# Modulation weights read by thirds: one ahead of each layer, two in the router stage and in the last attention

## The chip, the cores and the metric

The kernel runs on one core of a Trainium2 chip. The metric is the device time of one execution in microseconds (us), median of the runs. Engines work side by side, each through its own fixed list of instructions: PE (matmuls), DVE (vector), ACT (activations), POOL and SP, which here issue DMAs.

## The reference

Two transformer blocks on 256 tokens of width 1024, in fp32. The first mixes retention and sliding-window attention, then runs a mixture of 32 experts (top-1 group, top-2 experts) and a small gated embedding (PLE). The second block has two layers; each is modulated by a vector that comes from a condition c (for the tokens) and from c_ctx (for the context):

```
for i in range(DEPTH_2):
    mod = (s_c @ w_mod[i] + b_mod[i])[:, None, :]
    sh1, sc1, gt1, sh2, sc2, gt2 = jnp.split(mod, 6, axis=-1)
    ...
    h = modulate(rms_norm_2(x, g_norm1[i]), sh1, sc1)
    p = h @ w_in[i]
    ...  # three attention-like branches, merged to mix
    x_new = x + gt1 * mix
    x_new = x_new + gt2 * squared_relu_mlp(modulate(rms_norm_2(x_new, g_norm2[i]), sh2, sc2), ...)
```

w_mod[i] has 1024 rows and 6144 columns, 25 MB. Its first third of columns holds sh1 and sc1, needed at the start of a layer; the second gt1 (needed when the mixed branches are added) and sh2; the last sc2 and gt2, needed in the MLP.

## The kernel before

Weights are read from HBM by SP in pieces of up to 512 KB into a pool of 8 tiles called raw. Since products are made to fp32 accuracy, a piece is split by ACT (wh, L199) and DVE (wl, L200), three tiles each, and multiplied in three matmuls: L257 to L259 with 256 columns, L285 to L287 with 512. SP issues its loads in one order, and a load waits until its raw tile is free.

The instructions are written by Python code, and a list scheduler then fixes the order of each engine. A generator can be run beside the main code: `beside(steps, every)` (L202) enters it, each weight piece of the main code calls `advance` (L207), and one step is written for every `every` pieces; `drain` writes what is left. Pieces stand a little ahead in priority (AHEAD), modulation matmuls more (CLUSTER).

The modulation is such a generator, `w_mod` (L755). For each third of the columns it holds one PSUM tile of 512 columns and makes eight steps, one for each 128 rows: two raw tiles of 128x1024 are loaded (L764), and four matmuls (L769) multiply the two condition columns (padded to 32) with a quarter each, on a quarter of the array's columns each (`tile_position`). The weights are used as they are, without a split. A bias step (L775, L780) follows, then the copy out of PSUM and four small DMAs on POOL to a scratch in DRAM (modscr, L786). Once all thirds of a layer are there, two DMAs bring the columns back as modcol (L788). `rows` (in `Layer`) makes from modcol the gains A of both norms; `gate_row` reads gt1 and gt2 from modscr.

Stages in order: block1_mix and block1_out with w_out (the opening, with modulation of layer 0 beside block1_mix, one step for 1.25 pieces, PSUM tag cs); the router, and the start of the context layer `cl` (its projections na_k and na_v); the experts with the rest of the context layer; PLE and the attention of x0 (with all of layer 1's modulation beside them, every 1.5, later 2.5 pieces, tag pd); x0's MLP; x1's attention (the last attention) with the context's keys and values beside it; x1's output and MLP. In the attention, scores and transposes take PSUM tiles by turns from ps, cs and cd; dense products use pd and cd.

The router: w_out's residual gives x; L351 (ACT) sums its squares, Newton steps and L820 (DVE) make the normalised rows, L827 (PE) transposes them, L832 gives the logits; the choice of experts follows on DVE, then the lists for the scatter and gather on POOL, and L985 is the first transposition of gathered rows for an expert.

Of the kernel before, what the change touches and what calls it, by code (L numbers as in the profile page):

```python
# [15 lines left out]
ALU = mybir.AluOpType  # L16
# [51 lines left out]


WEIGHTS = (8, 3, 3)  # L70
MOD_EVERY = 1.25
AHEAD = 80
LANE = 192
EDGE = 160
# [3 lines left out]
KV_EVERY = 5.0  # L78
MOE_EVERY = 2.68
CTX_EVERY = (1.0, 1.2)  # L80
MOD1_EVERY = (1.5, 2.5)
CHAIN_EVERY = (1.0, 0.8)
ACTS_E = {"a8": 6, "a4": 6, "a2": 4, "tg": 2}
ACTS_C = {"a8": 4, "a4": 5, "a2": 3, "tg": 2, "pr": 1, "pt": 1, "lr": 1}
# [79 lines left out]
class Build:  # L164
# [252 lines left out]
    def run_all(self):  # L417
        nc, tc, i = self.nc, self.tc, self.i
        with ExitStack() as ctx:
            self.P = ctx.enter_context(tc.tile_pool(name="keep", bufs=1))  # L420
            self.W = ctx.enter_context(tc.tile_pool(name="weights", bufs=1))
            self.Dr = ctx.enter_context(tc.tile_pool(name="scr", bufs=1, space=DRAM))
            self.psum = ctx.enter_context(tc.tile_pool(name="psum", bufs=1, space=PSUM))
            self.ident = self.P.tile([128, 128], F32, name="ident")
            self.sums = self.P.tile([128, 2, 2, 2], F32, name="sums").rearrange("p s t c -> s p t c")
            self.ints = self.P.tile([128, 16], I32, name="ints")
            self.x = self.P.tile([128, 2, 1024], F32, name="xres")
            self.mod_input()
            for t in range(2):
                nc.sync.dma_start(self.x[:, t], i["x"][0, t * 128:t * 128 + 128])  # L430
            nc.sync.dma_start(self.ident, i["ident"])
            self.modcol = self.P.tile([128, 2, 2, 6, 8], F32, name="modcol")
            self.modscr = [self.Dr.tile([2, 6144], F32, name=f"modscr{l}") for l in range(2)]
            self.kvscr = [self.Dr.tile([128, 5120], F32, name=f"kvscr{l}") for l in range(2)]
            self.ctxscr = self.Dr.tile([128, 2048], F32, name="ctxscr")
            self.X = ctx.enter_context(tc.tile_pool(name="xT", bufs=1))
            ca = ctx.enter_context(ExitStack())
            self.slots = ca.enter_context(tc.tile_pool(name="slots", bufs=1))
            cl = Layer(self, None, 0, "ctx")
            with ExitStack() as ce:  # L440
                early = Stream(self, ce, "e", ACTS_E, ["pd"], ["ps", "cd"])
                mod = self.beside(self.w_mod(early, "cs", 0), MOD_EVERY)
                mh = self.block1_mix(early)
                self.layer_consts(early)
                self.gple = self.gain_col("ple_gate_norm_g")
                self.drain(mod)
                self.loads, self.ready = self.expert_loads(), []
                cl.rows(early)
                self.block1_out(early, mh)
                cl.turn(early)  # L450
            self.dump("x1", self.x)
            cs = Stream(self, ca, "c", ACTS_C, ["cd"], ["cs"])
            cl.st = cs
            with ExitStack() as cr:
                route = Stream(self, cr, "r", {}, ["pd"], ["ps"])
                self.router(route, cs)
                for _ in range(2):
                    self.fetch()
                cl.start()
            experts = self.beside(self.moe(cs), MOE_EVERY)  # L460
            cl.finish()
            self.drain(experts)
            self.dump("x2", self.x)
            self.mst = cs
            mod = self.beside(self.w_mod(None, "pd", 1), MOD1_EVERY[0])
            self.ple(cs)
            ca.close()
            st = Stream(self, ctx, "b", ACTS_B, ["pd", "cd"], ["ps", "cs"])
            self.mst = st
            mod[1] = MOD1_EVERY[1]  # L470
            self.dump("x3", self.x)
            for tag, n in (("ss1", 1), ("nm", 16), ("ny", 16), ("nt", 16)):
                st.small([128, n], tag=tag, bufs=2 if tag == "ss1" else 8)
            self.na_mask = st.pool.tile([128, 64], F32, name="namask")
            nc.sync.dma_start(self.na_mask, i["na_mask"])
            self.W2 = st.pool
            self.W2.tile([128, 1024], F32R, name="wh", tag="wh", bufs=1)
            st.pad(LANE)
            kv = Layer(self, st, 1, "kv")
            x0 = Layer(self, st, 0, "x")  # L480
            x0.rows(st)
            x0.turn(st)
            x0.start()
            x0.finish(lambda: self.drain(mod), kv)
            self.dump("x4", self.x)
            x1 = Layer(self, st, 1, "x")
            x1.rows(st)
            kv.na_v()
            x1.turn(st)
            kv.na_k_end()  # L490
            chain = self.beside(kv.mla_kv(), KV_EVERY)
            x1.start()
            self.drain(chain)
            x1.finish()

    def layer_consts(self, st):
        nc, i, P = self.nc, self.i, self.P
# [254 lines left out]
        self.one = self.P.tile([1, 32], F32, name="one32")  # L752
        nc.vector.memset(self.one, 1.0)

    def w_mod(self, st, tag, l):  # L755
        nc, i = self.nc, self.i
        mm = nc.tensor.matmul
        for j in range(3):
            ps = self.psum.tile([128, 512], F32, name=tag, tag=tag, bufs=2)
            for k in range(8):  # L760
                wt = [self.weight(0) for _ in range(2)]
                for u in range(2):
                    c = j * 2048 + u * 1024
# [9 lines left out]
            for u in range(2):  # L773
                c = j * 2048 + u * 1024
# [9 lines left out]
            for g in range(4):  # L784
                c = (4 * j + g) * 512
                nc.gpsimd.dma_start(self.modscr[l][:, c:c + 512], ev[32 * g:32 * g + 2])  # L786
        for r in range(2):
            nc.gpsimd.dma_start(self.modcol[:, l, r], self.modscr[l][r].rearrange("(a p k) -> p a k", a=6, k=8))  # L788

    def router(self, st, act):  # L790
        nc, i = self.nc, self.i
# [23 lines left out]
        r = self.newton(st, self.sumsq(st, self.x), 2, 1.0 / D)  # L815
        lgT = one.tile([36, 256], F32, name="lgT")
        lps = st.dense()
        xn = act.a(8).rearrange("p (t k q) -> p t k q", t=2, k=8)
        for t in range(2):
            nc.vector.scalar_tensor_tensor(xn[:, t], self.x[:, t].rearrange("p (q k) -> p k q", k=8), r[:, t:t + 1],  # L820
# [2 lines left out]
        for j in range(4):  # L823
            ps = st.small_ps().rearrange("p (k t) -> p k t", k=2)
            for kk in range(2):
                for t in range(2):
                    nc.tensor.transpose(ps[:, kk, t * 128:t * 128 + 128], xn[:, t, 2 * j + kk], self.ident)  # L827
            hT = act.a(2).rearrange("p (k t) -> p k t", k=2)
            self.evac(hT, ps)
            for kk in range(2):  # L830
                k = 2 * j + kk
                mm(lps[:36, :256], wr[:, k], hT[:, kk], start=k == 0, stop=k == 7)  # L832
        nc.vector.tensor_copy(lgT, lps[:36, :256])
        lg = one.tile([128, 2, 36], F32, name="lg")
        ps = st.small_ps()
        for t in range(2):
            nc.tensor.transpose(ps[:, t * 36:t * 36 + 36], lgT[:, t * 128:t * 128 + 128], self.ident[:36, :36])
        nc.vector.tensor_tensor(lg, ps[:, :72].rearrange("p (t e) -> p t e", t=2),
                                br[:, None, :].to_broadcast([128, 2, 36]), op=ALU.add)
        tl = lambda shape, nm, dt=F32: one.tile(shape, dt, name=nm)  # L840
        gl = tl([128, 2, 8], "gl")
        nc.vector.memset(gl, -3.0e38)
# [43 lines left out]
        mm(ps[:, 1], tri[:, 1], M[:, 0], start=False, stop=True)  # L886
        mm(ps[:, 2], tri[:, 1], M[:, 0], start=True, stop=False)
        mm(ps[:, 2], tri[:, 1], M[:, 1], start=False, stop=True)
        rank = tl([128, 3, 32], "rank")
        nc.vector.tensor_copy(rank, ps[:, 0:3])  # L890
        cmax = tl([128, 1], "cmax")
# [5 lines left out]
        for t in range(2):  # L897
            for k in range(2):
                nc.vector.tensor_tensor_reduce(out=junk, in0=oh[:, t, k], in1=rank[:, t], scale=1.0, scalar=0.0,
                                               op0=ALU.mult, op1=ALU.add, accum_out=rk[:, t, k:k + 1])  # L900
# [26 lines left out]
        for g in range(8):  # L927
            for t in range(2):
                mm(ps[:, g:g + 1], S[:, t, 4 * g:4 * g + 4].rearrange("p e s -> p (e s)"), tok[:, t:t + 1],
                   start=t == 0, stop=t == 1)  # L930
        self.sti = self.ints[:, 5:13]
        nc.vector.tensor_copy(self.sti, ps[:, :8])

# [279 lines left out]
class Layer:  # L1213
# [74 lines left out]
    def rows(self, st):  # L1288
        nc, l, b = self.nc, self.l, self.b
        self.load_x(st)  # L1290
        mc = self.mc = b.modcol[:, l, self.r]
        self.gna, self.gm, self.gmt, self.gqc = (z[:, l] for z in (b.gna, b.gm, b.gmt, b.gqc))
        self.rope = b.rope if self.mode == "x" else None
        A = self.A = b.X.tile([128, 2, 8], F32, name="modA", tag="modA", bufs=3)
        for c in range(2):
            nc.vector.scalar_tensor_tensor(A[:, c], mc[:, 3 * c + 1], 1.0, b.g12[:, l, c], op0=ALU.add, op1=ALU.mult)
        self.xn = b.norm_rows(st, self.x, stats=self.mode == "x")

    def turn(self, st):
# [391 lines left out]
    def ffn(self, meanwhile=None):  # L1691
        nc, i, st, b, l = self.nc, self.i, self.st, self.b, self.l
        xn = b.norm_rows(st, self.x, stats=True)
        self.gate_row(5)
        if meanwhile:
            meanwhile()
        xT = b.turn(st, xn, mod=(self.A[:, 1], self.mc[:, 3]))
# [52 lines left out]
```

## Time and profile before

| | us |
|---|---|
| median of 3 runs | 1927.31 (1920.61 to 1930.31) |
| profiled execution | 1928.43 |
| its span in the trace | 1926.7 |
| PE busy | 1796.3 (93%) |
| DVE busy | 1243.7 (65%) |
| ACT busy | 919.0 (48%) |

The rows further down come from the trace of that one execution. A row of a window gives the busy time of each engine in the stretch, then the mean granted clock of PE (1 is full), the mean busy share of the DMA engines and what they moved. A row of waits adds up the idle time of an engine that ended with a given releaser. Matmuls are pipelined, so their records overlap: the pitch, from one start to the next, is what counts.

### The profile page before, as it was taken

What the parts mean: (1) busy time and instruction counts of PE and PEld (TensorE: products, weight loads), DVE (VectorE), ACT (ScalarE), POOL (GpSimd) and SP (SyncE); (2) the same over time, 40 slices, a digit from 0 to 9 for tenths busy, and PEclk for the clock granted to TensorE, in tenths of its full rate; (3) what the DMA queues carried; (4) which work ended last, traced back from release to release, by engine and by line L of the source; (5) the groups of instructions that cost most, each with busy time, mean ns of one, the idle gap of its engine ahead of it and who ended that gap; (6) DMA issues with size and microseconds to landing.
All of it is one profiled execution on the core that took longest, in us unless ns stands there. A gap on an engine that the chain in (4) does not pass through costs nothing. (4 is left out here: it accounts for less than half of the span.)

```text
span 1926.7 us, 32421 instructions
## 1 busy us (share of the span) xinstructions
PE 1796.3 (93%) x12572; PEld 1478.0 (77%) x12572; DVE 1243.7 (65%) x2324; ACT 919.0 (48%) x1432; POOL 214.3 (11%) x209
## 2 busy tenths in 40 slices
PE   5999878999999999988999989999999899998998
PEld 3678856777786877665777878799988888787998
DVE  3554656664567544455768596766688886866665
ACT  3433534563345433344535455655456555555443
POOL 3000111000110101100121110011100200010110
PEclk9999988999999999999999999999999999998999
DMA  8789847889999999977787753555567645254652
GB/s 277 257 309 289 269 146 236 299 289 334 334 344 361 324 366 333 341 271 247 254 241 208 225 165 100 164 179 193 197 184 225 172 126 165 72 195 143 197 189 95
DMA packets 277172, 448.82 MB, mean 233 GB/s; under 512 B 35582, under 2 KB 182380, under 8 KB 276568
## 3 DMA queue, kind: packets, MB, share of 16 engines
q1 hardware_dynamic: 266344, 417.30, 64.7%
q0 software_dynamic: 10672, 29.43, 5.2%
q8 instruction: 99, 1.62, 0.3%
q14 instruction: 57, 0.47, 0.1%
HBM read 430.77 MB, written 15.86 MB: 232 GB/s over the span
## 5 line engine op out<-in xcount | busy, mean ns | idle before, releaser
L200 DVE TENSOR_TENSOR wl<-raw,wh 128x1024 fp32r<-128x1024 f32 (+2 forms) x484 | 614.7, 1273 | 361.5 <-ACT wh L199 204.8
L199 ACT ACTIVATE wh<-raw 128x1024 fp32r<-128x1024 f32 (+2 forms) x484 | 505.3, 1047 | 561.6 <-PE pd L258 116.2
L259 PE MATMUL pd<-xT,wl 128*128 128x256 f32 x384 | 109.9, 286 | 5.6 <-DVE wl L200 5.6
L258 PE MATMUL pd<-xT,wh 128*128 128x256 f32 x384 | 109.9, 286 | 0.0
L257 PE MATMUL pd<-xT,wh 128*128 128x256 f32 x384 | 109.6, 285 | 0.3 <-DVE b_a L339 0.3
L259 PE MATMUL pd<-e_a,wl 128*128 128x256 f32 x288 | 81.8, 284 | 0.5 <-DVE wl L200 0.5
L257 PE MATMUL pd<-e_a,wh 128*128 128x256 f32 x288 | 82.0, 285 | 0.0
L995 PE MATMUL ps<-ew,m_heT 128*32 128x256 f32 x1024 | 75.6, 384 | 6.7 <-DMA ew<-in_w_exp_up_dram 5.6
L258 PE MATMUL cd<-xT,wh 128*128 128x256 f32 x288 | 81.5, 283 | 0.0
L258 PE MATMUL pd<-e_a,wh 128*128 128x256 f32 x288 | 81.4, 283 | 0.0
L259 PE MATMUL cd<-xT,wl 128*128 128x256 f32 x288 | 81.2, 282 | 0.1
L257 PE MATMUL cd<-xT,wh 128*128 128x256 f32 x288 | 81.2, 282 | 0.0
L259 PEld LDWEIGHTS pd<-xT,wl 128*128 128x128 f32 x384 | 73.5, 191 | 8.9 <-DVE wl L200 6.4
L258 PE MATMUL cd<-b_a,wh 128*128 128x256 f32 x280 | 77.7, 277 | 0.0
L257 PE MATMUL cd<-b_a,wh 128*128 128x256 f32 x280 | 77.7, 277 | 0.0
L259 PE MATMUL cd<-b_a,wl 128*128 128x256 f32 x280 | 77.5, 277 | 0.0
L257 PEld LDWEIGHTS pd<-xT,wh 128*128 128x128 f32 x384 | 73.2, 191 | 4.3 <-issue 3.1
L258 PEld LDWEIGHTS pd<-xT,wh 128*128 128x128 f32 x384 | 73.3, 191 | 2.9 <-issue 2.5
L285 PE MATMUL cd<-wh,xT 128*128 128x512 f32 (+2 forms) x208 | 73.3, 354 | 0.0
L286 PE MATMUL cd<-wl,xT 128*128 128x512 f32 (+2 forms) x208 | 72.6, 349 | 0.1
L287 PE MATMUL cd<-wh,xT 128*128 128x512 f32 (+2 forms) x208 | 72.4, 348 | 0.0
L1669 POOL TENSOR_TENSOR xres<-xres,b_a 128x512 f32<-128x512 f32 x24 | 37.5, 1561 | 304.5 <-DVE b_a L1667 304.5
(774 smaller groups left out, 5087.6 us busy)
## 6 DMA issues: line engine op xcount, KB each, us to landing
raw<-in_ffn_w_dram SPq DMA_DIRECT2D x192, 512.0 KB, 4.4
raw<-in_w_in_dram SPq DMA_DIRECT2D x168, 512.0 KB, 5.0
raw<-in_w_mod_dram SPq DMA_DIRECT2D x96, 512.0 KB, 5.8
ew<-in_w_exp_gate_dram SPq DMA_DIRECT2D x64, 512.0 KB, 7.7
ew<-in_w_exp_up_dram SPq DMA_DIRECT2D x64, 512.0 KB, 8.4
ew<-in_w_exp_down_dram SPq DMA_DIRECT2D x64, 512.0 KB, 7.5
raw<-in_w_out_dram SPq DMA_DIRECT2D x32, 512.0 KB, 5.5
raw<-in_w_in_dram SPq DMA_DIRECT2D x16, 504.0 KB, 4.3
```

Of the source, the lines that this page charges most:

```text
L199: self.nc.scalar.activation(h, src, AF.Copy)
L200: self.nc.vector.tensor_tensor(l, src, h.bitcast(F32), op=ALU.subtract)
L257: mm(ps, wh[:, s], xh[:, k], start=k == 0, stop=False)
L258: mm(ps, wh[:, s], xl[:, k], start=False, stop=False)
L259: mm(ps, wl[:, s], xh[:, k], start=False, stop=k == n - 1)
L285: mm(ps[t], xh[:, k, s], wh, start=k == 0, stop=False)
L286: mm(ps[t], xh[:, k, s], wl, start=False, stop=False)
L287: mm(ps[t], xl[:, k, s], wh, start=False, stop=k == K - 1)
L995: mm(pg[32 * e:32 * e + 32, u * 256:u * 256 + 256], heT[:, kh * 4 + k, 32 * e:32 * e + 32], ws[e][:, k], start=kh == 0 and k == 0, stop=kh ...
L1669: (nc.vector if stats else nc.gpsimd).tensor_tensor(xs, xs, tmp, op=ALU.add)
```

## The change

w_mod takes a list of thirds, and brings each third's modcol back with two small DMAs of its own. For layer 0, the first third is made beside block1_mix (a step for 4 pieces) and the other two beside the router and the start of the context layer (a step for 2, tag pd), for which the router calls `advance` at six places; they are drained after `cl.start()`. For layer 1, the first third is made beside PLE and x0 (a step for 7, tag cs), the others beside x1's attention (a step for 4, tag cs), drained in x1.finish before the output. The second norm's gain A[:, 1] is made in `ffn`. Lines behind L441 shift by 1 to 9.

```diff
-MOD_EVERY = 1.25
+MOD0_EVERY = (4.0, 2.0)
-MOD1_EVERY = (1.5, 2.5)
+MOD1_EVERY = (7.0, 4.0)
...
-                mod = self.beside(self.w_mod(early, "cs", 0), MOD_EVERY)
+                mod = self.beside(self.w_mod(early, "cs", 0, (0,)), MOD0_EVERY[0])
...
+            self.mst = cs
+            mod = self.beside(self.w_mod(None, "pd", 0, (1, 2)), MOD0_EVERY[1])
             with ExitStack() as cr:
...
                 cl.start()
+            self.drain(mod)
...
-            self.mst = cs
-            mod = self.beside(self.w_mod(None, "pd", 1), MOD1_EVERY[0])
+            mod = self.beside(self.w_mod(None, "cs", 1, (0,)), MOD1_EVERY[0])
...
-            mod[1] = MOD1_EVERY[1]
...
+            mod = self.beside(self.w_mod(None, "cs", 1, (1, 2)), MOD1_EVERY[1])
             x1.start()
             self.drain(chain)
-            x1.finish()
+            x1.finish(lambda: self.drain(mod))
...
-    def w_mod(self, st, tag, l):
+    def w_mod(self, st, tag, l, thirds):
...
-        for j in range(3):
+        for j in thirds:
...
-        for r in range(2):
-            nc.gpsimd.dma_start(self.modcol[:, l, r], self.modscr[l][r].rearrange("(a p k) -> p a k", a=6, k=8))
+            for r in range(2):
+                nc.gpsimd.dma_start(self.modcol[:, l, r, 2 * j:2 * j + 2],
+                                    self.modscr[l][r, 2048 * j:2048 * j + 2048].rearrange("(a p k) -> p a k", a=2, k=8))
...
         lps = st.dense()
+        self.advance(4.0)
...
+            if j % 2:
+                self.advance(2.0)
...
+        self.advance(4.0)
         tl = lambda shape, nm, dt=F32: one.tile(shape, dt, name=nm)
...
+        self.advance(2.0)
         rank = tl([128, 3, 32], "rank")
...
+        self.advance(2.0)
         self.sti = self.ints[:, 5:13]
...
-        for c in range(2):
-            nc.vector.scalar_tensor_tensor(A[:, c], mc[:, 3 * c + 1], 1.0, b.g12[:, l, c], op0=ALU.add, op1=ALU.mult)
+        nc.vector.scalar_tensor_tensor(A[:, 0], mc[:, 1], 1.0, b.g12[:, l, 0], op0=ALU.add, op1=ALU.mult)
...
+        nc.vector.scalar_tensor_tensor(self.A[:, 1], self.mc[:, 4], 1.0, b.g12[:, l, 1], op0=ALU.add, op1=ALU.mult)
```

SP's order where w_out ends and the context's projections begin. Before (in_w_out is w_out, the tiles of 128x2x512 of in_w_in are na_k's, those of 336 na_v's, in_w_exp_gate an expert's):

```order
L241 DMA raw<-in_w_out_dram 128x2x512 x2
L947 DMA ew<-in_w_exp_gate_dram 128x1024
L241 DMA raw<-in_w_out_dram 128x2x512
L947 DMA ew<-in_w_exp_gate_dram 128x1024 x2
L241 DMA raw<-in_w_in_dram 128x2x512 x3
L947 DMA ew<-in_w_exp_gate_dram 128x1024
L241 DMA raw<-in_w_in_dram 128x2x512
L947 DMA ew<-in_w_exp_gate_dram 128x1024
L241 DMA raw<-in_w_in_dram 128x3x336 x2
```

And in the changed kernel:

```order
L241 DMA raw<-in_w_out_dram 128x2x512 x2
L766 DMA raw<-in_w_mod_dram 128x1024 x16
L241 DMA raw<-in_w_in_dram 128x2x512
L777 DMA raw<-in_b_mod_dram 1x1024 x2
L766 DMA raw<-in_w_mod_dram 128x1024 x2
L241 DMA raw<-in_w_in_dram 128x2x512 x2
L766 DMA raw<-in_w_mod_dram 128x1024 x2
L241 DMA raw<-in_w_in_dram 128x2x512
L241 DMA raw<-in_w_in_dram 128x3x336
```

Sixteen modulation tiles now stand behind w_out, and more of them between those of na_k and na_v; the experts' gate tiles stand earlier.

PE's order at the same place in the changed kernel (e_a is w_out's other operand, the L393 rows are transposes of the context, xT is the context for na_k):

```order
L285 MATMUL pd<-wh,e_a_1983 128x512
L771 MATMUL pd<-raw,sT 32x512 x16
L286 MATMUL pd<-wl,e_a_1983 128x512
L287 MATMUL pd<-wh,e_a_1984 128x512
L393 MATMUL cd<-ident,e_a_2064 128x128
L393 MATMUL ps<-ident,e_a_2064 128x128 x4
L393 MATMUL cd<-ident,e_a_2064 128x128 x3
L771 MATMUL pd<-raw,sT 32x512 x4
L393 MATMUL cd<-ident,e_a_2064 128x128
L393 MATMUL ps<-ident,e_a_2064 128x128 x4
L771 MATMUL pd<-raw,sT 32x512 x12
L285 MATMUL cd<-wh,xT 128x512 x2
```

All eight steps of the second third stand there ahead of na_k, four of them ahead of w_out's last two matmuls; before, no modulation matmul stood behind block1_mix until PLE.

PE's order in the last attention of the changed kernel, in a dense product (wh and wl against xT), as one step of the last third stands there:

```order
L257 MATMUL pd<-xT,wh 128x256
L771 MATMUL cs<-raw,sT 32x512
L258 MATMUL pd<-xT,wh 128x256
L771 MATMUL cs<-raw,sT 32x512
L259 MATMUL pd<-xT,wl 128x256
L771 MATMUL cs<-raw,sT 32x512
L257 MATMUL pd<-xT,wh 128x256
L771 MATMUL cs<-raw,sT 32x512
L258 MATMUL pd<-xT,wh 128x256
```

The four matmuls of the step stand one by one between dense ones. Before, no modulation matmul stood in this stage.

## Rows read from the trace of the kernel before

**Rows 1.** The page: busy time, slices of PE and its clock.

```profile
PE 1796.3 (93%) x12572; PEld 1478.0 (77%) x12572; DVE 1243.7 (65%) x2324; ACT 919.0 (48%) x1432; POOL 214.3 (11%) x209
...
PE   5999878999999999988999989999999899998998
...
PEclk9999988999999999999999999999999999998999
```

**Rows 2.** Windows of 50 us: engines' busy time, clock, DMA share, GB/s.

```profile
0.00:50.00 50.00, 29.18 (x138) 20.07 (x139) 18.89 (x48) 17.71 (x27) 18.07 (x31) 0.93 0.90 282
...
250.00:300.00 50.00, 40.15 (x199) 31.71 (x198) 31.43 (x91) 17.82 (x29) 6.83 (x12) 0.86 0.44 134
```

**Rows 3.** Windows of 10 us.

```profile
40.00:50.00 10.00, 7.91 (x42) 7.62 (x43) 6.11 (x16) 3.39 (x6) 0.00 (x0) 0.66 1.01 386
50.00:60.00 10.00, 7.89 (x51) 5.30 (x50) 6.24 (x27) 5.32 (x9) 0.00 (x0) 0.83 0.82 303
...
270.00:280.00 10.00, 2.98 (x10) 1.81 (x11) 6.51 (x14) 2.33 (x5) 1.08 (x2) 0.50 0.39 138
```

**Rows 4.** Timeline, router: start, length, instruction, [idle before <- what ended it].

```profile
267.92 0.76 ACT L199 ACTIVATE wh<-raw 128x672 fp32r<-128x672 f32 x1 [1.71 <-PE cd L287]
268.59 1.04 ACT L351 ACTIVATE r_junk<-xres 128x1024 bf16<-128x1024 f32 x1
...
273.45 4.03 DVE L820 SCALAR_TENSOR_TENSOR c_a<-xres,r_ny,c_a 128x1024 f32<-128x1024 f32 x2
...
275.71 0.66 PE L827 MATMUL ps<-ident,c_a 128*128 128x128 f32 x2 [7.83 <-issue]
...
314.68 1.73 PE L985 MATMUL ps<-ident,m_he 128*128 128x128 f32 x7 [3.37 <-DMA m_he<-xnscr,ints]
```

**Rows 5.** Window of the last attention.

```profile
1443.00:1711.00 268.00, 253.17 (x1858) 223.84 (x1859) 209.71 (x489) 150.39 (x271) 30.54 (x22) 0.97 0.54 157
```

**Rows 6.** PE's waits in the last attention: total, times, longest.

```profile
PE cs L1652 <- ACT b_a L337: 3.5, 1, 3.5
PE cd L1140 <- DVE b_a L200: 2.9, 1, 2.9
...
PE cs L1326 <- ACT b_a L404: 2.3, 1, 2.3
```

**Rows 7.** Timeline of PE: a whole step, then lone matmuls between dense ones.

```profile
102.92 1.06 PE L769 MATMUL cs<-raw,sT 128*32 128x512 f32 x8
103.92 0.39 PE L258 MATMUL pd<-e_a,wh 128*128 128x256 f32 x1
...
886.91 0.39 PE L287 MATMUL cd<-wh,ew 128*128 128x512 f32 x1
887.14 0.40 PE L285 MATMUL cd<-wh,ew 128*128 128x512 f32 x1
887.47 1.04 PE L769 MATMUL pd<-raw,sT 128*32 128x512 f32 x2
...
888.87 1.04 PE L769 MATMUL pd<-raw,sT 128*32 128x512 f32 x2
```

**Rows 8.** Windows of the modulation matmuls L769 alone.

```profile
0.00:200.00 200.00, 27.48 (x192) 3.95 (x192) 0.97 0.86 281
850.00:1100.00 250.00, 35.75 (x192) 5.19 (x192) 0.98 0.76 237
```

**Rows 9.** PE's waits in the opening.

```profile
PE pd L285 <- ACT wh L199: 6.4, 3, 3.8
PE cs L769 <- DMA raw<-in_w_mod_dram: 5.6, 3, 3.2
```

**Rows 10.** PE's waits from 840 to 1100 us.

```profile
PE ps L393 <- ACT b_a L380: 6.6, 1, 6.6
PE pd L769 <- DMA raw<-in_w_mod_dram: 5.6, 6, 1.5
...
PE cs L1171 <- DVE b_aden L1159: 1.2, 1, 1.2
```

## The prediction

> **What bounds the kernel now.** I read the page's first two parts, then the windows, then the waits by stretch, then the places in order of time. PE is busy 93% of the span and its row of slices is lowest in the first slice and the sixth, where the clock is lower too [rows 1]. So time is PE work plus the places where PE waits, and each stage has its own kind of wait. The opening (0 to 257 us, the end of w_out) is where loads are short: 29.18 of the first 50 us are PE work while the DMA engines are .90 busy [rows 2]. From 250 to 300 the DMA share is .44, and PE has 40.15 of 50 us [rows 2]; in the ten us from 270 PE works 2.98 at a clock of .50 [rows 3]. The gap there is not a load: the router's transposes L827 come at 275.71, since the sum of squares L351 runs on ACT only at 268.59, right behind the last split of na_v's first group, and the normalised rows L820 on DVE take 4.03 us from 273.45 [rows 4]. The first expert work, L985, is at 314.68 [rows 4]. In the last attention (1443 to 1711) PE works 253.17 of 268 us at DMA .54 [rows 5]: 14.8 us of idle time, in short waits of at most 3.5 us [rows 6], and much room for loads.
>
> **What a modulation step costs.** A step is two tiles of 512 KB and four matmuls, one for each quarter of the array's columns. Where the four stand in a row they run together: eight records (two for a matmul) of 1.06 us in all, and the next dense matmul starts 1.00 us after the first [rows 7]. Where one stands alone between dense matmuls of 512 columns, the period is 888.87 - 887.47 = 1.40 us, of which the dense one takes 0.23 (its pitch just before); 1.17 us are left for one matmul [rows 7]. So a step broken in four costs 4.7 us, not 1.05, and what counts is not the matmuls, whose number stays 216, but the runs in which they stand. I counted these runs in the order of both kernels (a run of n costs n/4, rounded up). Before: 28 for layer 0, all in the opening, and 37 for layer 1, beside PLE and x0; 65, where 54 is the least. After: 16 in the opening, 20 in the router stage, 20 beside PLE and x0, 42 in the last attention; 98. The busy time agrees: 27.48 us for the 24 steps of layer 0 (without bias), 35.75 for those of layer 1 [rows 8].
>
> The row that prices the lone matmul is 1.04 us long and takes 1.17 of the engine's time [rows 7], so 0.13 us go beside it. The Trainium skill, TensorEngine Tiling (Array Packing), Key Properties, says that a change of tiling mode drains the engine, which is what a lone matmul between full-width ones asks for twice. By that rule the 0.13 is paid for each run, by the record alone it would be free; the 34 broken runs in the last attention come to 40 us by the one and 35 by the other. I take the measured period. The trace agrees in sign, and no run here shows the drain by itself.
>
> **Opening: -27 us (-18 to -36).** PE loses 28 runs of 1.05 = 29.4 us and gets 16: 6 whole and 10 broken, 6 x 1.05 + 10 x 1.17 = 18.0; -11. The waits for modulation tiles, 5.6 us, go, and so does most of ACT's waiting for dense tiles that stood behind them in SP's queue, 6.4 us seen at L285 [rows 9]; -11. The clock was .66 from 40 to 50 us and .83 from 50 to 60 [rows 3], behind such waits, which is (1 - .66) x 10 + 1.7 = 5.1 us of full clock lost; -5. The upper end has the queue as the bound: 32 fewer tiles of 512 KB would be worth more than PE's share of them. The lower end leaves half the waits where they are, since dense loads also wait for each other.
>
> **Router stage: +25 us (+8 to +34).** Here the moved steps meet the one chain that starts the experts. The order of SP puts 16 modulation tiles right behind w_out and ahead of na_k's weights. Eight raw tiles exist and a modulation tile is free only after its matmuls, which stand at w_out's end, so the second eight and the nine tiles up to na_v's first group (25 up to there in all) come after it. A tile goes at 512 KB / 386 GB/s = 1.36 us in the fullest window [rows 3] and at 281 / .86 = 327 GB/s, 1.60 us, in the opening as a whole [rows 8]; I take 1.47. That is 17 x 1.47 = 25 us after w_out's end. ACT has L351 behind the splits of just these tiles, as before (order of ACT: four splits of na_k, one of na_v, then L351). From L351 to L827 it was 7.1 us [rows 4]; and DVE's Newton steps now share DVE with splits of na_v whose tiles come 2 to 6 later. So L827 comes 33 to 40 us after w_out's end, I take 36; it was 19. From L827 to L985 it was 39 us; 12 of the 20 runs now stand in that stretch, 13 us, of which the topk's idle time and the 3.37 us wait for the gathered rows [rows 4] hide a part; I take 46. The expert work then starts 36 + 46 = 82 us after w_out, where it was 58: +24, and +1 for the small transfers of POOL ahead of the router's scatter. Bounds: if the tiles all fit into the stretch's free DMA time (.56 of 50 us, 28 us, of the 47 us that 32 tiles take), only PE's 21 us less the 9 us gap are left, +12, less 4 for the clock; if nothing in the router hides any of it, 40 + 52 - 58 = +34. Layer 0 thus ends near zero: -2. The experts behind it are merely shifted.
>
> **PLE and x0: -18 us (-8 to -24).** Before, 37 runs: 23 x 1.05 + 14 x 1.17 = 40.5. After, 20, of which 4 are whole: 22.9. -17.6 of PE work. Waits for modulation tiles of 5.6 us [rows 10] shrink with two thirds of the tiles, -4; but the 6.6 us wait for a norm [rows 10] had a step just ahead of it that filled part, and its cover goes, +3.
>
> **Last attention: +43 us (+24 to +52).** 42 runs that were not there, 8 whole and 34 broken: 8.4 + 39.8 = 48 us. Of the 14.8 us of idle time [rows 5] the steps can fill only what lies behind them and ahead of the wait; the long waits are for ACT and DVE at small tiles (3.5, 2.9, 2.3 us [rows 6]), and the runs stand mostly inside dense stretches, far from them; I take 7 us off, of 0 to 15. Loads cost nothing here (17 MB at DMA .54); +2 for a late tile now and then (of 37 runs before, 6 waited, 5.6 us in all [rows 10]). The gate row of the output needs the last third's scratch, but its bias stands far ahead of w_out, so no wait there. The gain A[:, 1], now made in the FFN, is one small DVE row: nothing.
>
> **Sum.** 1928.4 (profiled run, 1.7 us above its span) - 27 + 25 - 18 + 43 = 1951.4; the median of the runs stands 1.1 us below that run: 1950.
>
> **Rivals.** (1) *The loads decide, not PE* (ends faster). If the opening is bound by SP's queue, 32 tiles fewer are worth up to 32 x 1.47 = 47 us, and with PE ready for four fifths of that -38, and the router stage takes them for +12 in its free DMA time. Layer 0 gives -26, layer 1 +25 with my terms; with all 14.8 us idle in the last attention filled, +17: 1927 - 9 = 1918, or 1912 with the upper end of PLE. It decides from where the experts start: under 290 us (it was 314.7). For: DMA .90 and PE 29.18 in the first 50 us. Against: L351 stands behind the splits.
> (2) *No change*: the router stage hides its steps as in (1), the opening gives my -27: 1928 - 15 + 25 = 1938, and with waits filled, 1925 to 1937.
> (3) *The score tiles wait* (slower still). The open sums of the third now hold one of the two "cs" PSUM tiles for eight steps, while the attention takes its scores and transposes by turns from ps, cs and cd. L1171 waited so once in the first attention, 1.2 us [rows 10]; some 20 such tiles at half of that or all of it are +12 to +24: 1962 to 1974. For: that sharing is new there. Against: those waits were rare, and dense matmuls stand between.
> (4) *It does not do what it says*: if broken steps overlapped with dense work, 42 runs would cost little; the period of 1.40 [rows 7] speaks against it. Held in (2).
>
> **How the numbers follow.** Forecast .56 (1938 to 1961); rival 3 .16; rival 2 .17; rival 1 .11. About 0.5%, 9.6 us, is what a measurement of this kernel can tell from no change. Within it (1918 to 1937) fall rival 2 and a little of the others: .19; faster .11; slower .70. The range leaves out the better part of rival 1 and the top of rival 3: 1919 to 1972.
>
> **What would show it.** w_out's end near 230; L831 (L827 before) some 36 us behind it; L994 (L985) near 312; the records of single modulation matmuls at 1.04 us; PE's work in the last attention near 301 us of 311. If the experts start before 295, the router term is wrong; if the last attention is longer by under 30 us, the price of a broken step is.

## The result, and the profile after

The changed kernel takes 1957.54 us (median of 6 runs) beside 1926.63 of the kernel before: ratio 1.0156, 95% interval 1.0134 to 1.0177, some 31 us slower. The forecast was 1950, slower, with a range of 1919 to 1972. The profiled execution took 1957.82 us, its span is 1956.0.

The same instructions of both traces, by their start in us, show where the time goes (the modulation itself left out; in the first line, where the order changed, it is the first row behind w_out's last matmul):

| place | before | after | shift | change in this stage | forecast |
|---|---|---|---|---|---|
| first row after w_out's last matmul | 256.73 | 230.10 | -26.6 | -27 | -27 |
| first expert transposes (L985, now L994) | 314.68 | 313.74 | -0.9 | +26 | +25 |
| last of the experts' stage | 813.02 | 820.15 | +7.1 | +8 | 0 |
| x0's MLP running | 1206.39 | 1192.41 | -14.0 | -21 | -18 |
| start of the last attention | 1438.90 | 1425.43 | -13.5 | +0.5 | 0 |
| end of it | 1722.25 | 1751.45 | +29.2 | +43 | +43 |

Windows of the changed kernel (columns as in [rows 2]): the 30 us behind w_out's end, and the last attention, which answers to [rows 5].

```profile
230.00:260.00 30.00, 21.11 (x99) 11.33 (x98) 11.24 (x16) 10.43 (x15) 5.19 (x9) 0.89 0.99 364
...
1429.00:1740.00 311.00, 299.62 (x2000) 230.82 (x2001) 212.32 (x492) 151.66 (x273) 38.64 (x34) 0.97 0.64 190
```

The last attention has 299.62 us of PE work where it had 253.17, in 311 us where it had 268: PE is its bound as before, and the work has grown. In the router stage the DMA engines are .99 busy in the 30 us behind w_out's end; in the kernel before, the same 30 us had .46:

```profile
256.73:286.73 30.00, 20.52 (x82) 13.90 (x81) 15.06 (x26) 10.31 (x15) 6.29 (x11) 0.77 0.46 143
```

The router's rows, to set beside [rows 4]:

```profile
255.70 1.05 ACT L199 ACTIVATE wh<-raw 128x1008 fp32r<-128x1008 f32 x1 [0.36 <-PE cd L287]
256.65 1.04 ACT L351 ACTIVATE r_junk<-xres 128x1024 bf16<-128x1024 f32 x1
...
267.82 0.66 PE L831 MATMUL ps<-ident,c_a 128*128 128x128 f32 x2 [6.66 <-issue]
```

L351 again stands right behind the split of na_v, now 26.6 us behind w_out's end (230.10) where it was 11.9, and L831 follows 37.7 us behind it. Modulation matmuls by place (opening, router stage, PLE and x0, last attention), to set beside [rows 8]:

```profile
0.00:200.00 200.00, 16.66 (x64) 2.22 (x64) 0.97 0.78 238
200.00:345.00 145.00, 19.38 (x128) 3.33 (x128) 0.93 0.80 276
850.00:1100.00 250.00, 16.83 (x64) 2.30 (x64) 0.96 0.65 188
1429.00:1740.00 311.00, 37.61 (x128) 5.21 (x128) 0.97 0.64 190
```

As many matmuls (64, x128 records) take 19.38 us in the router stage, where most steps are whole, and 37.61 in the last attention, where most are broken. A timeline of PE there (start, length, instruction), beside [rows 7]:

```profile
1639.11 0.38 PE L259 MATMUL cd<-b_a,wl 128*128 128x256 f32 x1
1639.42 1.04 PE L771 MATMUL cs<-raw,sT 128*32 128x512 f32 x2
1640.40 0.39 PE L257 MATMUL cd<-b_a,wh 128*128 128x256 f32 x1
1640.72 1.04 PE L771 MATMUL cs<-raw,sT 128*32 128x512 f32 x2
```

The period is 1.30 us with a dense matmul of 256 columns (its pitch at this clock is 0.12, as in the rows at the end of this document): 1.18 us for a lone modulation matmul, where the row of before, with a dense one of 512 columns, gave 1.17.

### The profile page after: what moved, and what is told of

It is laid out like the page before. It is cut to its first block, busy times and chain, and to the rows that moved or that the text cites. A ratio compares the mean times of both kernels' runs of the same rounds, so it can differ in the third digit from the quotient of the medians.

```text
span 1956.0 us, 32419 instructions
## 1 busy us (share of the span) xinstructions
PE 1833.1 (94%) x12572; PEld 1483.2 (76%) x12572; DVE 1247.2 (64%) x2323; ACT 916.8 (47%) x1432; POOL 221.7 (11%) x217
## 5 line engine op out<-in xcount | busy, mean ns | idle before, releaser
L771 PE MATMUL cs<-raw,sT 128*32 128x512 f32 x256 | 71.1, 619 | 10.7 <-DMA raw<-in_w_mod_dram 10.7
L285 PE MATMUL cd<-wh,xT 128*128 128x512 f32 (+2 forms) x208 | 72.8, 354 | 3.6 <-ACT wh L199 3.2
```

Of the source, the lines that this page charges most:

```text
L285: mm(ps[t], xh[:, k, s], wh, start=k == 0, stop=False)
L771: mm(ps[32 * g:32 * g + 32], self.sT[:, k], wt[u][:, v * 512:v * 512 + 512], start=k == 0, stop=False, tile_position=(0, 32 * g))
```

## The experiments

Times are medians beside runs of the kernel before on the same chip, with the ratio and its interval.

**The two layers apart.** l0_only undoes the change in layer 1, l1_only in layer 0.

```diff
# l0_only
-MOD1_EVERY = (7.0, 4.0)
+MOD1_EVERY = (1.5, 2.5)
...
-            mod = self.beside(self.w_mod(None, "cs", 1, (0,)), MOD1_EVERY[0])
+            mod = self.beside(self.w_mod(None, "pd", 1, (0, 1, 2)), MOD1_EVERY[0])
...
+            mod[1] = MOD1_EVERY[1]
...
-            mod = self.beside(self.w_mod(None, "cs", 1, (1, 2)), MOD1_EVERY[1])
...
# l1_only
-MOD0_EVERY = (4.0, 2.0)
+MOD0_EVERY = (1.25, 2.0)
...
-                mod = self.beside(self.w_mod(early, "cs", 0, (0,)), MOD0_EVERY[0])
+                mod = self.beside(self.w_mod(early, "cs", 0, (0, 1, 2)), MOD0_EVERY[0])
...
-            mod = self.beside(self.w_mod(None, "pd", 0, (1, 2)), MOD0_EVERY[1])
...
```

> Layer 0 of the changed kernel (first third in the opening, two in the router stage) with layer 1 as before. By the landmarks of the two traces w_out's end is 24 us earlier, and the experts start 3 us later and run 2 to 5 us longer: +5 us, 1931 (1927 to 1936). If the gain of the opening were kept to the end: 1903. If the router stage alone had caused the loss: 1950 or more.

> Layer 0 as before, layer 1 of the changed kernel (first third beside PLE and x0, two in the last attention). Theory P: 37 runs become 20 + 42 = 62: -21 beside PLE and x0, +43 in the last attention, +22 in all: 1949 (1943 to 1956). If the loss were the router stage's: 1905 to 1927.

l0_only: 1934.85 us, 1.0052 (1.0037 to 1.0066), +10 where 5 was expected, inside its range. l1_only: 1947.68, 1.0108 (1.0075 to 1.0141), +23 as expected. Two thirds of the loss come from layer 1, and the parts add up to the whole within what the runs tell (10 + 23 beside 31). Layer 0's opening is 21 us shorter in l0_only too (237.42 to 216.15), and all of it is gone when the experts run (4 to 7 us later than before from 350 us to their end). Behind them l0_only is 7 to 11 us later, with layer 1 as before; no run separates why.

**The broken steps.** A scheduler's priority decides whether the four matmuls of a step stay together. a_whole is the changed kernel, b_whole the kernel before, with that priority raised; no load changes its place in the code.

```diff
-CLUSTER = 160
+CLUSTER = 320
```

> The changed kernel with CLUSTER, the priority of the modulation matmuls, at 320 in place of 160: the scheduler then leaves the four matmuls of nearly every step together, 56 runs in place of 98, with the same loads at the same pace, the same PSUM tiles and the same stages. Theory P (a lone matmul costs 1.17 us of PE, a whole step 1.05): 42 runs fewer, 7 in the opening, 2 in the router stage, 11 beside PLE and x0, 22 in the last attention, 42 x 1.17 = 49 us of PE, of which some is given to waits: 1957.5 - 45 = 1912 (1904 to 1922); the last attention shrinks from 311 us to 287. Theory Q (the moved loads, their raw tiles and the queue cost the time): 1950 to 1957. Theory S (the held PSUM tile makes scores wait): 1950 to 1957 too.

> The kernel before with CLUSTER at 320: 54 runs in place of 65, none broken. Theory P: 11 x 1.17 = 13 us fewer, nearly all of it beside PLE and x0 (10 runs): 1913 (1908 to 1919). Theories Q and S: 1926, since no load moves.

a_whole: 1925.31, 0.9993 (0.9975 to 1.0010). One number gives back all 31 us, and the same number gives the kernel before nothing (b_whole: 1924.56, 1.0003, 0.9976 to 1.0029). So the broken steps are the cause of the loss, and not the places of the thirds by themselves. But the forecasts were missed: -45 for a_whole, -13 for b_whole. The last attention of a_whole is 30 us longer than that of the kernel before, in place of 43; 12 us went where 24 were expected. PE's work does shrink, as the windows of L771 alone (18.36 us where it took 37.61) and of the whole stage show:

```profile
1406.00:1709.00 303.00, 18.36 (x128) 2.89 (x128) 0.97 0.65 198
...
1406.00:1709.00 303.00, 278.36 (x2024) 230.48 (x2023) 217.81 (x499) 154.03 (x281) 39.53 (x35) 0.97 0.65 198
```

PE works 278.36 us where it worked 299.62, and its idle time grows from 11.4 to 24.6 us. What comes in place of the work are waits, here PE's in that stage (total, times, longest):

```profile
PE cs L771 <- DMA raw<-in_w_mod_dram: 8.5, 6, 2.3
PE cd L1149 <- DVE b_a L339: 5.3, 1, 5.3
PE ps L1180 <- DVE b_aden L1168: 4.3, 1, 4.3
```

In the changed kernel, with its broken steps, the longest waits were these, with 2.4 us for modulation tiles:

```profile
PE cd L1149 <- ACT b_qh L1389: 4.8, 1, 4.8
PE cs L771 <- DMA raw<-in_w_mod_dram: 2.4, 3, 1.3
```

In b_whole the waits for modulation tiles beside PLE and x0 grow from 5.6 [rows 10] to 9.8:

```profile
PE pd L769 <- DMA raw<-in_w_mod_dram: 9.8, 9, 3.0
```

So the price of a lone matmul was right and the sum made from it was not: PE reaches the next tile earlier and waits for it. In b_whole these 4 us of waits are not all of the 13. Its granted clock is lower too: .9729 in the mean of its ten runs, .9765 in the 24 runs of the kernel before beside them. By an estimate from these two, .0036 of 1925 us, that is up to 7 us; why the clock is lower, no run separates. a_whole and the changed kernel have the same mean clock, .973.

**The loads of the last attention.** noload_x1 is the changed kernel in which each moved third of layer 1 reads only its first pair of tiles.

```diff
-                wt = [self.weight(0) for _ in range(2)]
-                for u in range(2):
-                    ...
+                if k == 0 or not (l == 1 and j > 0):
+                    wt = [self.weight(0) for _ in range(2)]
+                    for u in range(2):
+                        ...
```

> The changed kernel without 14 of the 16 pairs of loads in the last attention: each third's first two tiles are used by all its eight steps (so layer 1's gate and MLP modulation are not the reference's). The matmuls stay; their order has 49 runs there in place of 42. Theory P (PE time of the runs): the last attention stays as long as in the changed kernel or grows by the 7 runs, 311 to 318 us, less the 2.4 us of waits for tiles: the whole at 1957 to 1965. Theory Q (loads and their slots): the last attention comes back towards its 268 us, to 280 or less: 1930 or less.

1965.77, 1.0202 (1.0134 to 1.0270, two runs): the 14 MB less of loads gain nothing, and the stage is 316 us long with 305.23 of PE work, at a DMA share of .50:

```profile
1429.00:1745.00 316.00, 305.23 (x1985) 229.48 (x1984) 212.53 (x488) 149.40 (x268) 37.57 (x34) 0.98 0.50 138
```

Seven more runs of modulation matmuls, some 6 us more of PE work. With broken steps the stage is PE's, and the loads have no visible part in it.

**The same with whole steps.** whole_noload1 is a_whole with only the first pair of each third of layer 1 read (the condition is `l == 1`), CLUSTER 640.

> The kernel with whole steps, without the loads of layer 1's modulation beyond each third's first pair of tiles (those two serve all eight steps, so layer 1's modulation is not the reference's); CLUSTER 640, 61 runs. a_whole took 1925 where the price of a broken step alone forecast 1912. If late modulation tiles and the raw tiles they hold took the other 13 us (waits of 1.8 us beside PLE and x0 and 8.5 in the last attention, and dense tiles behind them in the queue): 1908 to 1916. If the waits for ACT and DVE take PE's gain in any case: 1921 to 1927.

1907.75, 0.9886 (0.9854 to 0.9919, two runs). Against a_whole, 9 us are gone when x0's attention ends and 8.5 more at the end of the last attention, though it has 5 runs of modulation matmuls more. In the last attention PE's idle time is 17.0 us in place of 24.6, with a little more work:

```profile
1391.00:1690.00 299.00, 282.01 (x2051) 235.03 (x2050) 224.37 (x511) 156.71 (x285) 38.70 (x35) 0.98 0.54 154
```

So with whole steps the loads cost what was missing from the forecast of a_whole, 13 us. It is not shown in which way: the late tiles, the raw tiles they hold, which dense weights need too, and their place in the queue all went together, and the matmuls moved as well (28 of each of the last two thirds now stand in one row).

**Earlier loads.** whole_ahead has whole steps (CLUSTER 640, 55 runs), and each step loads the next step's tiles; DEEP is 1, and mod_tiles holds the loads of one step.

```diff
+                if k == 0:
+                    ahead = [self.mod_tiles(l, j, kk) for kk in range(DEEP)]
+                wt = ahead.pop(0)
+                if k + DEEP < 8:
+                    ahead.append(self.mod_tiles(l, j, k + DEEP))
```

> The kernel with whole steps, and each step's two tiles loaded one step earlier (so two of the eight raw tiles are held a step longer); CLUSTER 640, since with tiles at hand 320 leaves steps broken: 55 runs. If the late tiles, for which PE waited 10.2 us in the opening, 1.8 beside PLE and x0 and 8.5 in the last attention of a_whole, are what kept it from the forecast 1912: 1908 to 1918. Rival (dense tiles wait instead, with fewer raw tiles left for them, or the waits only move to ACT and DVE): 1922 to 1930.

1929.70, 1.0019 (0.9998 to 1.0040): no gain, the rival's time. Waits for modulation tiles fall from 8.5 to only 6.1 us in the last attention and from 10.2 to 3.7 in the opening, where a dense product now waits 8.3 us for ACT's rows:

```profile
PE pd L258 <- ACT e_a L568: 8.3, 1, 8.3
PE cs L780 <- DMA raw<-in_w_mod_dram: 3.7, 3, 1.6
```

**The router stage.** noload_router is the changed kernel with only the first pair of each of layer 0's moved thirds read (condition `l == 0 and j > 0`); late drops the calls of `advance` in the router, so that na_k's and na_v's tiles come ahead of most modulation tiles.

> The changed kernel without 14 of the 16 pairs of loads of layer 0's second and last third (each third's first two tiles serve all eight steps, so layer 0's gates and MLP modulation are not the reference's). The matmuls stay, in nearly as many runs. My theory of the router stage (the modulation tiles ahead of na_k's and na_v's, behind whose splits L351 stands, cost 17 us of the chain, PE's part the rest): L831 comes 19 to 24 us behind w_out's end in place of 37.7, the experts start 60 to 70 us behind it in place of 83.6: 1937 to 1945. Rival (PE's 20 us of modulation matmuls set the router's chain): L831 still 35 us or more behind, 1950 or more.

> The changed kernel without the calls of advance in the router, so that the steps of layer 0's second and last third are paced by the context layer's pieces alone and SP loads most modulation tiles between and behind those of na_k and na_v; all work stays. My theory: L831 comes 20 to 28 us behind w_out's end in place of 37.7, but the tiles then stand ahead of the experts' up and down tiles, so that a part comes back there: 1948 (1940 to 1957). Rival (the queue has to move the same bytes before the experts, in whatever order): 1957.

noload_router: 1944.47, 1.0089 (1.0063 to 1.0114), 13 us less than the changed kernel, as expected. L832 (the transposes) comes at 258.62, 29 us behind w_out's end at 229.3, between the changed kernel's 37.7 and the expected 19 to 24; the experts start at 305.82, 77 us behind (83.6 in the changed kernel), where 60 to 70 were expected. That PE's modulation matmuls, 32 of which now stand in one row ahead of na_k and take 7.1 us, keep part of the delay is likely, but not shown. late: 1959.28, 1.0167 (1.0116 to 1.0218), as the rival had it. Its chain is much shorter: L830 comes at 252.75, 25 us behind w_out's end, as expected, and the experts' L988 at 302.22, 11.5 us earlier than in the changed kernel. Nothing of that is left 50 us later: the row that stands at 356 us in the kernel before comes 4.5 us later than in the changed kernel. Two windows of late, and one of the kernel before, show the loads there:

```profile
290.00:314.00 24.00, 20.45 (x197) 11.72 (x195) 6.57 (x22) 5.00 (x18) 5.16 (x8) 1.00 1.01 386
300.00:340.00 40.00, 22.16 (x179) 10.01 (x178) 14.56 (x49) 9.31 (x21) 8.71 (x14) 0.77 0.99 369
...
300.00:340.00 40.00, 31.47 (x242) 22.75 (x242) 22.98 (x85) 16.10 (x38) 4.41 (x6) 0.87 0.80 269
```

In late the DMA engines are fully busy at 369 to 386 GB/s and PE works 22.16 of 40 us, where the kernel before (last row) had 31.47 at .80. So which tile stands first moves the start of the experts and not the end of the stage; the moved bytes come back a little later. That they alone take the gain is not shown: noload_router, without most of them, also loses 6.5 us between the experts' start and the row at 350 us of the kernel before.

**The held PSUM tile.** x1_pd takes the PSUM tile of the last attention's thirds from pd in place of cs.

```diff
-            mod = self.beside(self.w_mod(None, "cs", 1, (1, 2)), MOD1_EVERY[1])
+            mod = self.beside(self.w_mod(None, "pd", 1, (1, 2)), MOD1_EVERY[1])
```

> The changed kernel with the PSUM tile of the last attention's two thirds taken from pd, the dense products' tag, and not from cs. Theory S (scores and transposes wait for the held cs tile): 12 to 24 us come back, 1933 to 1946. Theory P: the order has 94 runs in place of 98, 4 x 1.17 = 5 us: 1953 (1950 to 1958).

1963.96, 1.0178 (1.0144 to 1.0211, two runs): not faster than the changed kernel (1.0156, 1.0134 to 1.0177), and nothing of the 12 to 24 us came back, so scores did not wait for the held cs tile to any such amount. Four runs of matmuls fewer should have given 5 us, and that was missed too: the last attention runs 5 to 8 us later than in the changed kernel, of which 4 us are there ahead of it (at 1399 us), and PE's waits for modulation tiles grew from 2.4 to 4.0.

**A kernel that beats both?** l1_whole keeps layer 0 as before and moves layer 1's thirds, with whole steps (l1_only with CLUSTER 320).

> Layer 0 as before, layer 1 by thirds as in the changed kernel, whole steps everywhere (56 runs). By the landmarks of a_whole and b_whole, layer 0 gives -2, PLE and x0 -33 and the last attention +30: 1922 (1917 to 1927), which the kernel before, at 1926, may or may not be told from. If moving the thirds is worth anything once the steps are whole, this is under 1917.

1928.83, 1.0007 (0.9984 to 1.0031), above the expected 1917 to 1927. Its trace gains 32 us up to the first low-rank transposes of x0's attention (1097.29 to 1065.12) and gives all of it back in the last attention. None of the kernels that do all the work is faster than the kernel before by more than the measurement tells.

## Why the prediction was right

**The counted runs** carried it. The price of a lone matmul, 1.17 us in [rows 7], came back as 1.18 in the changed trace. a_whole shows it from the other side: with 56 runs in place of 98, the loss is gone.

**Opening, -27**: -26.6, but not by the terms that I gave, so the sum is in part luck. PE's work fell by 19.2 us, although four steps that were counted in the router stage (3.6 us) stand ahead of w_out's end, and its idle time by 7.4:

```profile
0.00:256.73 256.73, 222.00 (x1517) 176.64 (x1517) 134.14 (x281) 105.10 (x164) 40.86 (x60) 0.95 0.84 274
...
0.00:230.10 230.10, 202.76 (x1392) 169.01 (x1393) 126.06 (x268) 97.93 (x153) 36.35 (x52) 0.98 0.78 233
```

I had 11 us of waits in the sum, and the wait for modulation tiles did not go: PE stood once for 7.6 us, in place of three waits of 5.6 in sum. ACT's missing dense tiles at L285 went from 6.4 to 0.3, as said. Here PE's waits of the changed opening, beside [rows 9]:

```profile
PE cs L771 <- DMA raw<-in_w_mod_dram: 7.6, 1, 7.6
PE pd L285 <- ACT e_tg L731: 1.6, 1, 1.6
...
PE pd L285 <- ACT wh L199: 0.3, 1, 0.3
```

The clock's 5 us came, but from another place. From 40 to 60 us the changed kernel lost as much as before, behind its one long wait (.50 and .98, 5.2 us of full clock); what it gained lies mostly from 220 to 250 us, where the kernel before had .78, .88 and .83, and it had 1.00 in the 50 us ahead of w_out's end (the rows of 40 to 60 and of 180 to 230 are of the changed kernel, those of 220 to 250 of the kernel before):

```profile
40.00:50.00 10.00, 5.65 (x24) 3.59 (x24) 4.41 (x19) 4.64 (x10) 0.00 (x0) 0.50 0.90 238
50.00:60.00 10.00, 8.98 (x73) 7.71 (x73) 5.99 (x27) 6.17 (x21) 0.00 (x0) 0.98 1.01 347
...
220.00:230.00 10.00, 5.71 (x24) 4.04 (x23) 7.61 (x17) 7.40 (x10) 1.27 (x1) 0.78 0.90 312
230.00:240.00 10.00, 9.33 (x44) 7.54 (x43) 4.39 (x5) 4.50 (x6) 2.48 (x3) 0.88 0.84 227
240.00:250.00 10.00, 8.74 (x31) 7.02 (x32) 7.02 (x12) 5.51 (x9) 0.00 (x0) 0.83 0.57 181
...
180.00:230.00 50.00, 45.92 (x295) 38.20 (x294) 26.80 (x36) 20.94 (x25) 8.67 (x8) 1.00 0.72 204
```

**Router stage, +25**: +26, and its terms in size as well: L831 37.7 us behind w_out (36), the experts 83.6 (82). That the tiles in front cost a part of it is shown by noload_router (8 us of its 13 are there when the experts start). That their place decides the start of the experts is shown by late, and that it decides the time is not: late moved them behind and the time stayed.

**The experts, 0**: +8. This term was missing: I had the experts "merely shifted". PE's idle time from their start to their end rose from 15.2 to 21.0 us:

```profile
314.68:813.02 498.34, 483.10 (x3801) 368.07 (x3805) 278.11 (x463) 215.51 (x335) 48.19 (x46) 0.99 0.92 329
...
313.74:820.15 506.41, 485.36 (x3804) 370.24 (x3805) 280.37 (x469) 216.17 (x339) 53.03 (x52) 0.99 0.91 330
```

It is 17.2 to 21.2 in seven other kernels that move layer 0's thirds (30.5 in late) and 14.2 to 16.3 in the three that do not (b_whole, l1_only, l1_whole). So some 4 to 5 us of the 8 belong to the change. Most of them lie in the first 40 us, where transposes of the context wait for DVE:

```profile
PE cs L1512 <- DVE c_a L1557: 4.0, 1, 4.0
```

What delays these rows, no run separates; the rest is likely what two executions differ by: l0_only, x1_pd and noload_x1, with the same layer 0, lose 3.5 to 4.2 us in this stretch.

**PLE and x0, -18**: -21. Dropping 17 runs and the tiles was worth a little more than the sum.

**Last attention, +43**: +43, in PE's work (+46, where 48 was in the sum) and not in waits. The idle time fell by 3.4 us, from 14.8 to 11.4, where the sum had 5 off (7 filled, 2 for late tiles). noload_x1 shows no part of the loads in it.

**The forecast of 1950** was 7.5 us too low. By the traces the stages add up to +29 where they were forecast at +23: the experts' 8 us that were missing, less the 3 that PLE and x0 gave more, and a little of each other term. Rival 1 (loads decide the opening) is wrong for this kernel; with whole steps loads do cost time, as whole_noload1 shows. Rival 2 failed on the router: the stage does not hide its steps. Rival 3 fell with x1_pd, and rival 4 with the 46 us of PE work. What the Trainium skill, TensorEngine Tiling (Array Packing), Key Properties, says of a drain at a change of mode agrees with the 0.13 us that lie beside each lone record; for the 34 broken runs of the last attention that is 4.4 us. No run here shows the drain by itself.

**What was wrong came after it**: the expectations of a_whole and b_whole took PE's saving as time. It is only a saving while the next tile is there and the clock stays.

## What to carry to other kernels

Count how the instructions of a small packed product stand in the engine's order, since four matmuls that use a quarter of the array each took 1.05 us in a row here and 4.7 once other work came between them. Moving PE work from one stage bound by PE to another one gained nothing by itself, and loads moved out of a stage have to fit in front of the next consumer of the queue. When a saving on one engine is forecast, ask which transfer it will meet next.

## What the runs showed of the hardware

A short wait can be followed by a slower clock. In a_whole PE waited 2.30 us for a tile, until 1611.50. Some 1.5 us later the dense matmuls went from a pitch of 0.12 us to one of 0.21; the mean granted clock of the 4 us from 1613 was .57, with most of them at the lower of the two levels, 1.2 GHz.

```profile
1611.50 1.07 PE L771 MATMUL cs<-raw,sT 128*32 128x512 f32 x8 [2.30 <-DMA raw<-in_w_mod_dram]
...
1612.71 0.28 PE L257 MATMUL cd<-b_a,wh 128*128 128x256 f32 x1
1612.83 0.28 PE L258 MATMUL cd<-b_a,wh 128*128 128x256 f32 x1
...
1613.33 0.41 PE L258 MATMUL cd<-b_a,wh 128*128 128x256 f32 x1
1613.54 0.41 PE L259 MATMUL cd<-b_a,wl 128*128 128x256 f32 x1
```

The window of the 4 us behind it:

```profile
1613.00:1617.00 4.00, 4.00 (x23) 4.00 (x23) 3.01 (x7) 0.84 (x1) 2.01 (x1) 0.57 0.54 141
```

Not every such wait was followed by it: behind PE's wait of 2.17 us that ended at 1077.57 in the same trace, the next 7 us had full clock.

```profile
1077.00:1085.00 8.00, 6.08 (x49) 5.63 (x50) 8.00 (x31) 3.15 (x4) 3.03 (x6) 1.00 0.69 198
```
